# The products of all head chains taken in steps between runs of 24 dense products, with the key norms, decay and rate as a chain of their own

## The chip, the cores and the metric

The kernel runs on one core of a Trainium2 chip. The metric is the device time of one execution in microseconds (us). Engines are named as in the profile: PE is TensorE (matrix products), PEld its weight loads, DVE VectorE, ACT ScalarE, POOL GpSimd, SP SyncE (which here issues the weight transfers). Each engine executes its own instructions strictly in the order in which the program lists them, and waits at an instruction until the data that it names are there.

## The reference

A batch of 256 tokens of width 2048 passes through two transformer blocks in fp32. The first block puts 16 meta tokens in front (T = 272 tokens) and is the one that matters here:

```
proj = rms(h) @ w_in
z_rwkv, z_fox, z_gate = split(proj)
z_rwkv = z_rwkv + (shift(z_rwkv) - z_rwkv) * mu
y_a = rwkv7(z_rwkv, ...)       # 16 heads of 64
y_b = fox(z_fox, ...)          # 16 heads of 64
merged = sig(g_a) * (y_a @ w_a) + sig(g_b) * (y_b @ w_b)
h = h + merged @ w_o
h = h + (silu(gate) * up) @ w_dn
```

rwkv7 is a recurrence over time with a 64x64 state S per head:

```
decay = exp(-exp(-softplus(-(w0 + tanh(wd) @ w2)) - 0.5))
a = sigmoid(a0 + ad @ a2)                     # the rate
kk = (k * k_k) / |k * k_k|                    # keys, normed per head
kf = k * (1 + (a - 1) * k_a)
S = S * decay + (S @ -kk) (kk * a)^T + v kf^T ;  y = S @ r
y = groupnorm(y) + sum(r * kf * r_k) * v ;  y_a = y * (sigmoid(gd) @ g2)
```

fox is causal attention with normed queries and keys and a forget gate that is summed over time and added to the scores before the softmax. The second block (a long convolution, latent attention and another gated feed-forward) isn't touched by the change.

## The kernel before

**Dense products.** Tokens lie along the free axis and features on the partitions. A dense output block (128 features by 256 to 272 tokens) is the sum of 16 k-steps. Each fp32 weight block of 128x128 is split into a high part `wh` and a low part `wl`, and the activations into `xh` and `xl`, so that one k-step is three products (`mm3`, L216 to L218: wh by xh, wl by xh, wh by xl) into one PSUM bank. Weights stream from memory in pieces of eight blocks of 128x128 (one 512 KB transfer on SP's queue into `wr`; ACT copies it to `wh`, L192; DVE subtracts to make `wl`, L193). Each of the three has three buffers.

**Heads.** `phase_heads` makes, for j from 0 to 7, the three projections k, v, r of RWKV head pair j and then its chain (`rwkv_pair`); then fk, fq, fv of fox pair j-1 and its chain (`fox_pair`); and some of the 32 gate blocks (`gate`), by the table GATES_PER_PAIR. The weights come in that order (`in_order`).

The RWKV chain works in five chunks of 64 tokens. From the projections come `p`, `lerp_d` and the shifted `kz`, `zv`, `zr` (L1034 to L1037). The decay and the rate come from two small products on the inputs `twh` and `adh` with weights from `lora` (tiles `sg`, `av`, L1133; the running sum `cc`, L1136; its exponentials `ee` and `ep`, L1140 and L1141), the key norm from a `headsum` (a sum over the 64 rows of a head as a product with a block matrix `bo` or `bm`, L296 and L297; its input is split into a high part `rs_r` on ACT and a low part `rs_q` on DVE). From them DVE makes `kk`, `bk`, `kf`, `ar` (L1149 to L1161) and `t`, which goes into a second headsum, of r, kf and r_k; its result becomes `bv` (L1167). Then come the products of `ar` and `bk` (L1178), the inverse of a triangular matrix in steps of doubling size (L1229, L1235, and `y`/`y5`, L1249 to L1259), and the walk over the five chunks: `rhs` (L1267 to L1271), `uv` (L1274 to L1276), the state `st` (L1280 to L1285) and the output `yc` (L1289 to L1291), with a group norm behind it (two more headsums). All these products are small: 32, 64 or 128 rows and columns of the array, so the array is used in several configurations.

**What sets the order.** The kernel is written one chain after the other. The scheduler of the tile framework lays the instructions of all chains and the dense products out on each engine by readiness and priority; the weight transfers and splits have a raised priority. Nothing in the code says after how many dense products a chain's product comes.

## Time and profile before

| | |
|---|---|
| median of 3 runs | 2821.36 us (2817.64 to 2821.42) |
| profiled execution, its own time | 2817.87 us |
| its span | 2816.1 us |
| mean granted clock of PE | 0.998 |
| PE busy | 2792.4 us (99%), 23296 instructions |
| PEld busy | 2634.0 us (94%) |
| DVE busy | 1845.4 us (66%) |
| ACT busy | 1346.6 us (48%) |
| chain of waits that ended last | PE 95%, DMA 2%, DVE 2%, ACT 1% |

The heads phase is about the first 790 us of the span. Products on PE overlap, so a product's duration (0.28 us for a dense one) isn't what it costs: that is the distance from its start to the next one's start. On DVE and ACT neighbouring instructions overlap by some hundredths of a microsecond, and the durations nearly add up. An execution time is 1.8 us longer than its span in the profile.

### The profile page before, as it was taken

What the parts mean: (1) busy time and instruction counts of PE and PEld (TensorE: products, weight loads), DVE (VectorE), ACT (ScalarE), POOL (GpSimd) and SP (SyncE); (2) the same over time, 40 slices, a digit from 0 to 9 for tenths busy, and PEclk for the clock granted to TensorE, in tenths of its full rate; (3) what the DMA queues carried; (4) which work ended last, traced back from release to release, by engine and by line L of the source; (5) the groups of instructions that cost most, each with busy time, mean ns of one, the idle gap of its engine ahead of it and who ended that gap; (6) DMA issues with size and microseconds to landing.
All of it is one profiled execution on the core that took longest, in us unless ns stands there. A gap on an engine that the chain in (4) does not pass through costs nothing.

```text
span 2816.1 us, 56217 instructions
## 1 busy us (share of the span) xinstructions
PE 2792.4 (99%) x23296; PEld 2634.0 (94%) x23296; DVE 1845.4 (66%) x2958; ACT 1346.6 (48%) x1994; POOL 143.2 (5%) x294
## 2 busy tenths in 40 slices
PE   9999999999999999999999999999999999999998
PEld 9988888888999999999999999999999999998886
DVE  8857667676576665555655556787777777775444
ACT  7545555655444544444444445444454444444443
POOL 0000000010000200000000000000100000000000
PEclk9999999999999999999999999999999999999999
DMA  7333333334576556555556666544555555566554
GB/s 247 128 109 114 105 110 114 104 108 138 180 251 212 193 191 194 194 192 194 194 194 202 201 200 213 165 147 149 190 187 195 194 193 193 195 193 225 193 194 164
DMA packets 147740, 497.13 MB, mean 177 GB/s; under 512 B 16251, under 2 KB 30940, under 8 KB 146908
## 3 DMA queue, kind: packets, MB, share of 16 engines
q1 hardware_dynamic: 128448, 458.42, 49.8%
q10 hardware_dynamic: 18396, 33.03, 3.4%
q8 instruction: 182, 2.98, 0.4%
q0 software_dynamic: 640, 2.10, 0.3%
q14 instruction: 74, 0.61, 0.1%
HBM read 478.27 MB, written 15.20 MB: 175 GB/s over the span
## 4 chain that ended last, share of the span: by engine, by line
PE 95%; DMA 2%; DVE 2%; ACT 1%; issue 0%; DVEq 0%; POOL 0%; ACTq 0%; POOLq 0%
PE psd L218 12%; PE psd L216 12%; PE psd L217 12%; PE psa L217 5%; PE psb L218 5%; PE psb L216 5%; PE psa L218 5%; PE psb L217 5%; PE psa L216 5%; PE psc L217 4%; PE psc L218 4%; PE psc L216 4%; PE psa L962 1%; PE psa L963 1%; PE psa L961 1%; PE psd L963 1%
## 5 line engine op out<-in xcount | busy, mean ns | idle before, releaser
L193 DVE TENSOR_TENSOR wl<-wr,wh 128x1024 fp32r<-128x1024 f32 (+1 forms) x872 | 1062.6, 1219 | 624.3 <-ACT wh L192 623.4
L192 ACT CAST wh<-wr 128x1024 fp32r<-128x1024 f32 (+1 forms) x872 | 908.5, 1042 | 1145.7 <-PE psd L218 328.5
L218 PE MATMUL psd<-xl,wh 128*128 128x256 f32 (+2 forms) x1280 | 370.4, 289 | 0.0
L216 PE MATMUL psd<-xh,wh 128*128 128x256 f32 (+2 forms) x1280 | 369.4, 289 | 0.0
L217 PE MATMUL psd<-xh,wl 128*128 128x256 f32 (+2 forms) x1280 | 368.0, 287 | 0.4 <-DVE wl L193 0.4
L218 PEld LDWEIGHTS psd<-xl,wh 128*128 128x128 f32 x1280 | 240.6, 188 | 7.7 <-issue 2.3
L217 PEld LDWEIGHTS psd<-xh,wl 128*128 128x128 f32 x1280 | 240.7, 188 | 6.6 <-issue 2.2
L216 PEld LDWEIGHTS psd<-xh,wh 128*128 128x128 f32 x1280 | 240.6, 188 | 6.3 <-issue 1.8
L216 PE MATMUL psd<-x3h,wh 128*128 128x256 f32 x496 | 140.3, 283 | 1.6 <-DVE yy L631 1.6
L218 PE MATMUL psd<-x3l,wh 128*128 128x256 f32 x496 | 140.4, 283 | 0.0
L217 PE MATMUL psd<-x3h,wl 128*128 128x256 f32 x496 | 138.6, 279 | 0.0
L216 PE MATMUL psd<-x4h,wh 128*128 128x256 f32 x368 | 100.8, 278 | 3.2 <-ACT x4h L252 3.2
L217 PE MATMUL psd<-x4h,wl 128*128 128x256 f32 x368 | 101.6, 277 | 0.0
L218 PE MATMUL psd<-x4l,wh 128*128 128x256 f32 x368 | 101.2, 277 | 0.0
L262 POOL TENSOR_TENSOR acc<-acc,ssq 128x256 f32<-128x256 f32 x42 | 58.4, 1391 | 822.6 <-ACT ssq L264 818.2
L217 PE MATMUL psa<-x4h,wl 128*128 128x256 f32 x352 | 97.4, 278 | 0.1
L218 PE MATMUL psa<-x2l,wh 128*128 128x256 f32 x352 | 97.4, 277 | 0.0
L216 PE MATMUL psa<-x2h,wh 128*128 128x256 f32 x352 | 97.4, 277 | 0.0
L216 PEld LDWEIGHTS psd<-x3h,wh 128*128 128x128 f32 x496 | 93.1, 188 | 4.5 <-issue 2.8
L218 PE MATMUL psb<-x2l,wh 128*128 128x256 f32 x352 | 97.2, 276 | 0.0
L217 PE MATMUL psb<-x2h,wl 128*128 128x256 f32 x352 | 97.2, 276 | 0.0
L216 PE MATMUL psb<-x2h,wh 128*128 128x256 f32 x352 | 97.2, 276 | 0.0
(673 smaller groups left out, 8384.2 us busy)
## 6 DMA issues: line engine op xcount, KB each, us to landing
wr<-w_in_dram SPq DMA_DIRECT2D x230, 512.0 KB, 3.4
wr<-w_gu_dram SPq DMA_DIRECT2D x176, 512.0 KB, 3.3
wr<-w_down_dram SPq DMA_DIRECT2D x176, 512.0 KB, 3.5
wr<-w_up_dram SPq DMA_DIRECT2D x176, 512.0 KB, 4.3
wr<-w_ab_dram SPq DMA_DIRECT2D x32, 512.0 KB, 4.3
wr<-w_o_dram SPq DMA_DIRECT2D x32, 512.0 KB, 3.4
wr<-w_out_dram SPq DMA_DIRECT2D x32, 512.0 KB, 4.2
spill_g<-acc ACTq DMA_DIRECT2D x32, 128.0 KB, 2.8
```

The costliest lines, as they stand in the source:

```text
L192: self.nc.scalar.copy(hi, src)
L193: self.nc.vector.tensor_tensor(out=lo, in0=src, in1=hi.bitcast(F32), op=ALU.subtract)
L216: nc.tensor.matmul(out, lhsT=wh, rhs=xh, start=start, stop=False)
L217: nc.tensor.matmul(out, lhsT=wl, rhs=xh, start=False, stop=False)
L218: nc.tensor.matmul(out, lhsT=wh, rhs=xl, start=False, stop=stop)
L262: nc.gpsimd.tensor_tensor(out=acc, in0=acc, in1=self.pending[id(acc)], op=ALU.add)
L961: nc.tensor.matmul(ps[b], lhsT=hh[:, k, bs], rhs=wh[:, q], start=k == 0, stop=False)
L962: nc.tensor.matmul(ps[b], lhsT=hh[:, k, bs], rhs=wl[:, q], start=False, stop=False)
L963: nc.tensor.matmul(ps[b], lhsT=hl[:, k, bs], rhs=wh[:, q], start=False, stop=k == HT - 1)
```

## The change

Every chain becomes a generator that stops at each place where a product would have to wait for another engine. `dense` counts k-steps, and after every TICK = 8 of them (24 dense products) it calls `tick`, which lets every live chain take one step. An `issue_after` holds these steps behind the dense product that was just written, and a `hold` keeps the next dense product behind all of them. So PE's order is written out: 24 dense products, one step of each chain, 24 dense products, and so on. The chains are:

- `rwkv_early` (new): the key norm, the two products for decay and rate (now in bank "a", not "b"), and the exponentials. It starts with the k projection of its pair, ahead of v and r.
- `rwkv_pair`: the rest; it starts behind the r projection. The transposes of `zv` come at its start. Where each chunk had the product of `ka` with `v` accumulate with that of `ar` and the state in one bank, the products of all five chunks are now made at once, copied by ACT into `kv` (L1342), and DVE adds `kv` to the state's product (L1385) where it copied before. `outer` (the product for `yc`) comes one step later.
- two `headnorm` chains per fox pair and `fox_heads`; the products with `v` move a step later, into bank "a".

`headsum` takes its bank itself and stops between the split of its input and its two products: for one step, or for two with gap=1 (the key norm and fox norms; the sum that makes `bv` and the two of the group norm have no gap). GATES_PER_PAIR goes from (2, 0, 2, 3, 3, 2, 2, 2, 0) to (5, 2, 3, 2, 3, 2, 3, 5, 0), and the weight stream with it. The forget gates move behind the last gate block of j = 0.

```diff
+TICK = 8
     def dense(self, out, st, kt, xh, xl, tok):
         for k in range(kt):
             wh, wl = next(st)
-            self.mm3(out, wh, wl, xh[:, k, tok], xl[:, k, tok], k == 0, k == kt - 1)
+            with ExitStack() as held:
+                for i in self.hold:
+                    held.enter_context(self.tc.issue_after(i))
+                m = self.mm3(out, wh, wl, xh[:, k, tok], xl[:, k, tok], k == 0, k == kt - 1).ins
+            self.hold = []
+            self.since += 1
+            if self.chains:
+                self.hold = [m]
+                if self.since >= TICK:
+                    self.since = 0
+                    self.tick(m)
+
+    def tick(self, ins):
+        for c in list(self.chains):
+            with self.tc.issue_after(ins):
+                if next(c, self) is self:
+                    self.chains.remove(c)
+        traced = self.nc.cur_bb.bb.instructions
+        at = next(k for k in reversed(range(len(traced))) if traced[k] is ins)
+        self.hold = [i for i in traced[at:] if i.engine == ins.engine]
...
-    def headsum(self, ps, w, src, n, pool=None):
+    def headsum(self, bank, w, src, n, pool=None, gap=0):
         self.split(src, hi, lo)
+        for _ in range(gap + 1):
+            yield
+        ps = self.ps(bank)[:, :n]
         self.nc.tensor.matmul(ps, lhsT=w, rhs=hi, start=True, stop=False)
         self.nc.tensor.matmul(ps, lhsT=w, rhs=lo, start=False, stop=True)
+        return ps
...
         nc.vector.scalar_tensor_tensor(out=t1[:, 64:], in0=zr[:, 64:], scalar=self.col("r_k", j), in1=kf[:, 64:], op0=ALU.mult, op1=ALU.mult)
-        ps = self.ps("b")[:, :S]
-        self.headsum(ps, self.bo, t1[:, 64:], S)
+        yield
+        for c0, n in ((0, 3), (3, 2)):
+            ps = self.ps("a").rearrange("p (c x) -> p c x", c=4)
+            for c in range(n):
+                nc.tensor.transpose(ps[:, c], zv[:, 64 * (c0 + c) : 64 * (c0 + c) + 128], self.con("ident"))
+            nc.scalar.copy(uv[64:128, c0 : c0 + n], ps[64:128, :n])
+            nc.vector.tensor_copy(v0[:64, c0 : c0 + n], ps[64:128, :n, 0:64])
+        ps = yield from self.headsum("b", self.bo, t1[:, 64:], S)
...
+            if c:
+                yield
+                rhs = self.tl(w2, [P, 64], "rhs")
+                ps = self.ps("c")
+                for hs in hss:
+                    nc.tensor.matmul(ps[hs, :64], lhsT=ar[hs, c, 0], rhs=st[hs], start=True, stop=True)
+                nc.vector.tensor_tensor(out=rhs, in0=ps[:, :64], in1=kv[:, c], op=ALU.add)
+                if c > 1:
+                    outer(c - 1, old)
+                yield
+                inner(c, rhs)
```

Below are the places at which the order of the engines changes most for what follows. Rows stand in an engine's order; names are tiles, with their buffer numbers.

**The headsum of r, kf and r_k in pair 2.** Its input is `t`, split into `rs_r` and `rs_q`; `psb` takes the sum. First PE before: the product of the low part stands 15 rows behind that of the high part (the first row).

```order
L296 MATMUL psb_2449<-rs_r_2450,bo_472 128x256
...
L216 MATMUL psd_3941<-xh_94,wh_3973 128x256
L217 MATMUL psd_3941<-xh_94,wl_3974 128x256
L297 MATMUL psb_2449<-rs_q_2451,bo_472 128x256
L1274 MATMUL psc_1780<-rhs_1778,xtf_1594 64x64 x2
L218 MATMUL psd_3941<-xl_95,wh_3973 128x256
```

And DVE before, up to that low part:

```order
L1163 SCALAR_TENSOR_TENSOR t_489_2439<-zr_48_431,cols_61,kf_2440 128x256
L1192 TENSOR_SCALAR bs_2489<-bk_2437,ed_2490 128x128 x4
L193 TENSOR_TENSOR wl_4026<-wr_4024,wh_4025 128x8x128
L193 TENSOR_TENSOR rs_q_2451<-t_489_2439,rs_r_2450 128x256
L1271 COPY rhs_1778<-psc_1773 128x64
```

Now PE has the same two products directly behind the state product L1384 of another pair's walk:

```order
L219 MATMUL psd_2641<-xl_95,wh_2693 128x272
L1384 MATMUL psc_2702<-st_2654,ar_1559 64x64 x2
L334 MATMUL psb_2706<-rs_r_2667,bo_472 128x256
L335 MATMUL psb_2706<-rs_q_2668,bo_472 128x256
L217 MATMUL psd_2641<-xh_94,wh_2693 128x272
```

And DVE now:

```order
L1256 COPY v_482_2628<-psa_2662 64x128
L1097 SCALAR_TENSOR_TENSOR zr_48_431<-lerp_d_2623,cols_61,p_2622 128x256
L1420 TENSOR_TENSOR yc_1524<-yc_1524,psc_2575 128x256
L1385 TENSOR_TENSOR rhs_2701<-psc_2702,v_258_1557 128x64
L194 TENSOR_TENSOR wl_2790<-wr_2788,wh_2789 128x8x128
L1247 TENSOR_TENSOR ar_2630<-zr_48_431,ee_2459 128x5x64
L1249 SCALAR_TENSOR_TENSOR t_485_2631<-zr_48_431,cols_61,kf_2632 128x256
L194 TENSOR_TENSOR rs_q_2668<-t_485_2631,rs_r_2667 128x256
L1259 TENSOR_TENSOR bv_2709<-psb_2706,zv_47_430 128x256
```

The low part `rs_q` moved from ahead of `rhs` to four rows behind it, and `rhs` reads the product (`psc_2702`) that stands directly ahead of the headsum on PE. In pairs 1 to 7 the row ahead is such a reader of the same step each time: `rhs` in pairs 1, 2, 4 and 6, the state `st` in pairs 3, 5 and 7.

**ACT at the end of a matrix inverse.** Before (pairs 4 and 5), the copy of `y` stands between the tanh of `sg` and of `av`:

```order
L1275 COPY uv_4656<-psc_4835 64x64
L1133 ACT_TABLE_LOAD
L1133 ACTIVATE sg_441<-psb_5686,half_427 128x272
L1252 COPY y_988_4807<-psa_4806 32x128
L1133 ACTIVATE av_442<-psb_5692,half_427 128x272
L1141 ACTIVATE ep_5702<-cc_5698 128x320
L192 CAST wh_6471<-wr_6470 128x8x128
L1140 ACTIVATE ee_5701<-cc_5698 128x640
L1259 COPY xtf_4689<-psa_4818 32x4x32
```

Now (pairs 3 and 4), the copies `kv` (named `v` here, L1342) and `y` stand behind all of the next pair's early chain:

```order
L355 ACTIVATE rs_r_4634<-rs_v_4633 128x320
L1421 DMA spill_ya<-yc_3612 128x256
L193 CAST wh_5664<-wr_5663 128x256
L356 ACTIVATE rs_q_4635<-rs_r_4634 128x320
L1215 ACT_TABLE_LOAD
L1215 ACTIVATE av_442<-psa_4648,half_427 128x272
L1223 ACTIVATE ep_4658<-cc_4654 128x320
L1222 ACTIVATE ee_4657<-cc_4654 128x640
L193 CAST wh_4811<-wr_4810 128x8x128
L193 CAST gh_5701<-wr_5700 128x256
L1342 COPY v_713_3754<-psc_4698 128x320
L1350 COPY y_919_4711<-psa_4710 32x128
```

And on PE their readers (L1365 needs `kv`, L1355 needs `y`) stand one run of 24 dense products behind the step that made those copies' inputs:

```order
L219 MATMUL psd_4688<-xl_95,wh_4744 128x258
L1365 MATMUL psc_4764<-v_713_3754,xtf_4068 64x64 x2
L1355 MATMUL psa_4752<-xtf_4068,y_919_4711 32x32 x8
L217 MATMUL psd_4688<-xh_94,wh_4744 128x258
```

So `kv` and `y` moved on ACT from the middle of the next pair's tanh and exponentials to behind them and behind two weight splits, and the next step on PE reads them. Pairs 0, 1, 3 and 5 have this overlap with the next pair's early chain.

**The start, pair 0.** Here the headsum of the key norm and that of r, kf and r_k are 23 dense products apart on PE now (from the first row to the last but one):

```order
L335 MATMUL psb_694<-rs_q_651,bo_472 128x320
L217 MATMUL psd_654<-xh_94,wh_686 128x258
...
L219 MATMUL psd_766<-xl_95,wh_813 128x256
L334 MATMUL psb_821<-rs_r_787,bo_472 128x256
L335 MATMUL psb_821<-rs_q_788,bo_472 128x256
```

DVE has 17 rows between the result of the first (`rs_v`) and the low part for the second (`rs_q_788`), of which these are the last twelve:

```order
L194 TENSOR_TENSOR wl_895<-wr_893,wh_894 128x8x128
L1097 SCALAR_TENSOR_TENSOR zr_48_431<-lerp_d_748,cols_61,p_747 128x256
L1241 TENSOR_TENSOR t_126_756<-kk_697,av_442 128x320
L1246 SCALAR_TENSOR_TENSOR ar_755<-kk_697,ee_722 128x5x64
L1247 TENSOR_TENSOR ar_755<-zr_48_431,ee_722 128x5x64
L1242 TENSOR_TENSOR bk_754<-t_126_756,ep_723 128x5x64
L1243 TENSOR_SCALAR t_126_756<-av_442,cols_61 128x320
L1244 SCALAR_TENSOR_TENSOR kf_757<-t_126_756,kz_46_429 128x320
L1245 TENSOR_TENSOR bk_754<-kf_757,ep_723 128x5x64
L1249 SCALAR_TENSOR_TENSOR t_126_756<-zr_48_431,cols_61,kf_757 128x256
L1271 TENSOR_SCALAR bs_831<-bk_754,ed_832 128x128 x4
L194 TENSOR_TENSOR rs_q_788<-t_126_756,rs_r_787 128x256
```

Before, the scheduler had put 13 us of the trace between these two headsums (65.07 to 78.78 us of the span, from the product of the first to the split for the second).

More of the change, by code (lines that the diff above doesn't have):

```diff
@@ L234, in dense, with chain, drain @@
             wh, wl = next(st)
-            self.mm3(out, wh, wl, xh[:, k, tok], xl[:, k, tok], k == 0, k == kt - 1)
+            with ExitStack() as held:
[17 more added lines that the diff above has]
+        self.hold = [i for i in traced[at:] if i.engine == ins.engine]
+    def chain(self, c):
+        next(c)
+        self.chains.append(c)
+        return c
+    def drain(self, chains):
+        for c in chains:
+            for _ in c:
+                pass
+            if c in self.chains:
+                self.chains.remove(c)
     def group(self, out, st, kt, xh, xl, toks, bring):
@@ L511, in headnorm @@
         nc.scalar.activation(out=sq, in_=z, func=AF.Square)
-        ps = self.ps("b")[:, :n]
-        self.headsum(ps, self.bo, sq, n, w)
+        ps = yield from self.headsum("b", self.bo, sq, n, w, gap=1)
         zn = self.tl(w2, [P, T], tag + "n")[:, :n]
@@ L1086, in phase_heads @@
             self.fox_setup(pr)
+            pairs, fox = [], None
             for j in range(9):
                 if j < 8:
[L1089 to L1091 removed]
+                    box = self.rwkv_inputs(j)
+                    self.drain(pairs[-2:-1])
+                    pairs.append(self.chain(self.rwkv_pair(j, w, box)))
                 if j:
[L1093 to L1095 removed]
+                    if j == 1:
+                        with self.tc.issue_after(behind):
+                            self.forget_gates()
+                    self.drain(fox)
+                    fox = [self.fox_pair(j - 1)]
+                else:
+                    fox = []
+                for i in range(GATES_PER_PAIR[j]):
+                    behind = self.gate().ins
             while self.ngate < 32:
                 self.gate()
+            self.drain(list(self.chains))
     def gate_inputs(self):
@@ L1244, in rwkv_pair @@
                 nc.gpsimd.tensor_copy(xf[:, 0], xt[:, 0])
+        yield
+        ps = self.ps("c")[:, : NC5 * 64].rearrange("p (c t) -> p c t", c=NC5)
+        for c in range(NC5):
+            for h, hs in enumerate(hss):
+                kat, vv = (ka[:, c], v0[:64, c]) if h == 0 else (gs[1][64:128, c, 0], uv[64:128, c, 64:128])
+                nc.tensor.matmul(ps[hs, c], lhsT=kat, rhs=vv, start=True, stop=True)
+        kv = v0
+        nc.scalar.copy(kv, ps)
         ps = self.ps("a")[:, :P].rearrange("p (c t) -> p c t", c=4)
```

163 lines of the change are left out of this document (92 added, 71 removed).

## The prediction

> **What bounds the kernel now.** I read the page's busy shares first, then the chain of waits, then busy time by stretch, to see whether PE has any room in the heads phase.
>
> ```profile
> PE 2792.4 (99%) x23296; PEld 2634.0 (94%) x23296; DVE 1845.4 (66%) x2958; ACT 1346.6 (48%) x1994; POOL 143.2 (5%) x294
> PE 95%; DMA 2%; DVE 2%; ACT 1%; issue 0%; DVEq 0%; POOL 0%; ACTq 0%; POOLq 0%
> ```
>
> ```profile
> core 0: us, PE busy (x) PEld busy (x) DVE busy (x) ACT busy (x) POOL busy (x), PEclk, DMA share, GB/s
> 30.00:70.00 40.00, 40.00 (x329) 39.92 (x328) 36.70 (x69) 30.82 (x44) 1.04 (x7) 1.00 0.62 200
> ...
> 70.00:200.00 130.00, 129.67 (x1223) 115.89 (x1224) 88.98 (x184) 63.99 (x114) 11.34 (x17) 1.00 0.36 118
> 200.00:500.00 300.00, 300.00 (x2798) 259.27 (x2797) 211.56 (x484) 162.45 (x315) 22.77 (x34) 1.00 0.34 111
> 500.00:800.00 300.00, 299.60 (x2691) 265.89 (x2691) 193.50 (x400) 162.18 (x293) 22.63 (x24) 1.00 0.45 144
> ```
>
> PE never stands still in the phase: 0.7 us of idle time in the 730 us from 70 to 800, at a granted clock of 1.00. The change can therefore gain only by making PE's own sequence shorter, and whatever it makes PE wait is lost one for one. DVE is busy for 65 to 70% of each stretch (91% in the first), so it has slack on average, and none to spare for a wait of a fixed length.
>
> What PE spends beyond products shows in PE's timeline around one visit to the chains:
>
> ```profile
> 301.16 0.28 PE L217 MATMUL psd<-xh,wl 128*128 128x258 f32 x1
> 301.28 0.28 PE L218 MATMUL psd<-xl,wh 128*128 128x258 f32 x1
> 301.49 0.27 PE L1267 MATMUL psc<-v,ka 64*64 64x64 f32 x1
> ...
> 303.91 0.29 PE L297 MATMUL psb<-rs_q,bo 128*128 128x272 f32 x1
> 304.04 0.28 PE L216 MATMUL psd<-xh,wh 128*128 128x258 f32 x1
> ```
>
> A dense product costs 0.12 us from start to start (301.16 to 301.28); going from it to a 64*64 product costs 0.21 (to 301.49). A headsum, 128*128 like the dense ones, is left for 0.13. So what costs is the change of the array's shape, about 0.09 us on entry. The Trainium skill ("TensorEngine Tiling (Array Packing)", Key Properties) says that switching the tiling mode drains TensorE; the rows agree, with 0.09 us as the price here. By that rule too the change gains only by its count of switches.
>
> **The change part by part.** *Fewer visits.* The order of PE's instructions has 282 runs of dense products before and 154 now, 146 of them of exactly 24; changes of array shape fall from 853 to 721. The number of dense and of chain products stays (4032 and 1729). 132 changes fewer at 0.09 us would be 12 us. Half of them are ways back, and the one that the rows show costs 0.01 (0.13 for 0.12): 66 x 0.09 + 66 x 0.01 = 7. I take -8 us, with -6 and -12 as ends.
>
> *Pinned places.* Before, a chain's product stood wherever its data were ready. Now it stands 24 dense products (24 x 0.12 = 2.9 us) and a step's small products behind the last one, ready or not. What DVE and ACT must do between two steps has to fit into that. The durations, with the groups of DVE and ACT from 70 to 786 us:
>
> ```profile
> L193 DVE TENSOR_TENSOR wl<-wr,wh 128x1024 fp32r<-128x1024 f32 (+1 forms) x154 | 185.0, 1201 | 61.0 <-ACT wh L192 60.3
> L1271 DVE COPY rhs<-psc 128x64 f32<-128x64 f32 x40 | 8.8, 220 | 14.2 <-PE psc L1269 12.7 <-PE psc L1267 0.9
> L1161 DVE TENSOR_TENSOR ar<-zr,ee 128x320 f32<-128x320 f32 x7 | 3.4, 479 | 0.6 <-ACT ee L1140 0.6
> L1163 DVE SCALAR_TENSOR_TENSOR t<-zr,cols,kf 128x256 f32<-128x256 f32 x8 | 3.8, 477 | 0.0
> L193 DVE TENSOR_TENSOR rs_q<-t,rs_r 128x256 fp32r<-128x256 f32 x8 | 3.3, 413 | 0.0
> L1285 DVE SCALAR_TENSOR_TENSOR st<-st,ed,psc 128x64 f32<-128x64 f32 x24 | 6.7, 278 | 6.8 <-PE psc L1280 6.3
> L1192 DVE TENSOR_SCALAR bs<-bk,ed 128x128 f32<-128x128 f32 x32 | 7.0, 277 | 0.0
> ```
>
> ```profile
> L192 ACT CAST rs_r<-t 128x256 fp32r<-128x256 f32 x8 | 3.2, 403 | 3.4 <-DVE t L1163 3.2 <-ACT uv L1275 0.2
> L1133 ACT ACT_TABLE_LOAD x4 | 5.1, 1283 | 0.1
> L1133 ACT ACTIVATE av<-psb,half 128x272 f32<-128x272 f32 x7 | 3.4, 483 | 0.2
> L317 ACT ACTIVATE rs_q<-rs_r 128x256 f32<-128x256 f32 (+2 forms) x31 | 13.4, 433 | 0.6
> L1141 ACT ACTIVATE ep<-cc 128x320 f32<-128x320 f32 x7 | 3.3, 471 | 3.5 <-DVE cc L1136 3.4
> L1140 ACT ACTIVATE ee<-cc 128x640 f32<-128x640 f32 x7 | 5.1, 732 | 0.0
> L192 ACT CAST wh<-wr 128x1024 fp32r<-128x1024 f32 (+1 forms) x153 | 156.0, 1021 | 121.9 <-PE psd L218 109.8 <-issue 6.1 <-DMA wr<-w_in_dram 2.7
> L1240 ACT COPY xt<-psa 128x320 f32<-128x320 f32 x24 | 10.3, 427 | 7.8 <-DVE xn L1237 7.4
> L1252 ACT COPY y<-psa 32x128 f32<-32x128 f32 x8 | 2.1, 259 | 0.3
> ```
>
> *(a) The headsum of r, kf and r_k, pairs 1 to 7.* It has no gap, and DVE's rows in the changed order show the trouble: the low part it needs stands behind `rhs`, and `rhs` reads the product directly ahead of it on PE. So PE finishes L1384 and then waits while DVE does `rhs` 0.22, a weight split 1.20, `ar` 0.48 and `t` 0.48, ACT the high part 0.40, DVE the low part 0.41: 3.2 us, with no room for anything beside. Four pairs (1, 2, 4, 6) are so. In pairs 3 and 5 it is `st` 0.28, four `bs` 1.11, a split 1.20 and 0.41: 3.0 us (the high part lies beside). In pair 7 `st`, a split and the low part: 1.9 us. Sum 4 x 3.2 + 2 x 3.0 + 1.9 = 20.7, say +21 us. Before, the same rows cost PE nothing, because the low part's product stood behind other dense products:
>
> ```profile
> 299.34 1.22 DVE L193 TENSOR_TENSOR wl<-wr,wh 128x1024 fp32r<-128x1024 f32 x1
> 300.48 0.87 DVE L1192 TENSOR_SCALAR bs<-bk,ed 128x128 f32<-128x128 f32 x4
> ...
> 301.68 0.41 DVE L193 TENSOR_TENSOR rs_q<-t,rs_r 128x256 fp32r<-128x256 f32 x1
> ```
>
> Here neighbours start 5 to 10% closer than their durations add up to (1.14 for 1.22), so the lower end is 18. The upper end has DVE late at `rhs` too, by one more weight split in each pair: 21 + 7 x 1.2 = 29. What is late behind it is the next weight split, which the wait itself gives time for.
>
> *(b) `kv` and `y`, pairs 0, 1, 3 and 5.* From the tanh of `sg` to the copy of `y` ACT has in order: tanh 0.48, table 1.28, root 0.47 (put at that of `ep`, of the same shape), a small split 0.40, the second part of the root 0.43, table 1.28, tanh 0.48, exponentials 0.47 and 0.73, a weight split 1.02, a small split 0.40, `kv` 0.43 (as the copy of the same shape at L1240), `y` 0.26: 8.1 us. PE comes back for it after two runs of dense products and one step, 5.8 + about 1 = 6.8 us. DVE's half of `y` is later still: behind the second tanh (4.8 us in) it has `av`, `kk` twice, `p`, `lerp_d`, `t` and `ar`, seven rows that I put at `ar`'s 0.48 at most (3.2 together, with `av` shorter), then a weight split 1.20 and `y` 0.28, which ends at 9.5. That makes 1.3 to 2.7 us each; I take 2, +8 us; the ends are 0 (a table load that is not needed, a split done earlier) and 12.
>
> *(c) The start, pair 0.* The headsums of key norm and of r, kf, r_k are 23 dense products apart, 2.8 us. The trace of before has the same work on DVE:
>
> ```profile
> 65.07 0.31 PE L297 MATMUL psb<-rs_q,bo 128*128 128x320 f32 x1
> ```
>
> ```profile
> 65.42 0.49 DVE L315 TENSOR_SCALAR rs_v<-psb 128x320 f32<-128x320 f32 x1 [1.03 <-PE psb L297]
> 65.97 1.23 DVE L193 TENSOR_TENSOR wl<-wr,wh 128x1024 fp32r<-128x1024 f32 x1
> 68.26 0.49 DVE L321 SCALAR_TENSOR_TENSOR rs_q<-rs_q,rs_v 128x320 f32<-128x320 f32 x1 [1.06 <-ACT rs_q L317]
> ...
> 78.78 0.41 DVE L193 TENSOR_TENSOR rs_q<-t,rs_r 128x256 fp32r<-128x256 f32 x1
> ```
>
> It took 14.1 us (65.07 to 79.19). Three fewer weight splits lie between now (3 x 1.14 = -3.4), none of the next pair's six input rows (6 x 0.4 = -2.4), and three such rows for `zr` come in (+1.2): 9.5, less the 2.8 that PE has: 6.7. I take +7 us, with 4 and 9 as ends.
>
> *Parts I cost at nothing.* The kat-by-v products at once and `kv`'s copy are the same products and one ACT copy in (b). Two more table loads (54 for 52 in the order of ACT) are 2.6 us on ACT, busy for half of the phase. The new order of gates moves weights that arrive well ahead; SP has no other work in between, and the transfers of 512 KB keep their count. If that cover were gone, each late piece would cost one split, 1.2 us.
>
> *Sum.* -8 + 21 + 8 + 7 = +28 us on the profiled execution of 2817.87 (span 2816.1 and 1.8 around it): 2846. The median before, 2821.36, is 3.5 above its profiled execution; I set the median of the changed kernel 2 above mine: 2848 us.
>
> **The rivals.** *Waits hidden, only the switches count (faster).* The steps would meet their data as before, and the -8 us would stand alone: 2821 - 8 = 2813. Place: the seven headsums of (a). For it: DVE is idle for a third of the phase. Against it: the order on DVE is fixed, and the row ahead reads PE's product of the same step, so no idle time before it helps. It decides if each wait in (a) is below 1 us with (b) and (c) near nothing.
>
> *Gain and waits cancel (same).* (a) at 1.2 us each, one split, because `ar` and `t` find their inputs early and the splits overlap: 7 x 1.2 = 8, against -8, with (b) and (c) near zero: 2821. For it: `t` itself doesn't need the split. Against it: the split stands ahead of it in DVE's order.
>
> *The clock drops (slower by more).* Each of some eight waits of over 3 us would let PE go on at half pace for a while; a run of 24 dense products at half pace costs another 2.9 us: 8 x 2.9 = 23, so 2871. Against it: the granted clock is 1.00 in every stretch above, but none has a wait as long. The Trainium skill ("TensorE: Matmul & The Clock Gate", Part 1) says that about 3.4 us of idle time bring the clock to half rate, and as long a busy time brings it back; by it (c) alone surely qualifies and those of (a) are at the edge. No run here shows it.
>
> *The ticks don't do what they say.* If order on PE were not held, times would stay within 0.2%; the 146 runs of exactly 24 speak against it, so I fold it into "same".
>
> **How the numbers follow.** Forecast 0.72; clock drop 0.12; same 0.08; hidden 0.08. The forecast's ends: all terms at their lowest, -12 + 18 + 0 + 4 = +10, give 2828 to 2830; all at their highest, -6 + 29 + 12 + 9 = +44, give 2862 to 2864. The range 2824 to 2866 holds these with 2 to 4 us for the spread of runs; the clock case and most of the two others lie outside. A change of 0.2% (5.6 us) is about what a measurement of this kernel can tell from none: slower by more than that 0.84 (forecast and clock drop), within it 0.08, faster 0.08.
>
> **What would show it.** In the profile after, PE's idle time between 30 and 790 us rises from below 1 us to about 36. In the groups, L335 on `rs_q`/`bo` (or L334) shows some 20 us of idle time ahead with DVE's or ACT's split as its releaser, L1355 or L1365 some 8 with `y`, `xtf` or `v0`. The start shows one wait of about 7 us near 60 to 75 us. Entries into 64*64 products still cost 0.21, and are fewer. DVE and ACT busy time stay within 1%. I am wrong if PE stays above 99.5% busy in the phase, if the idle time is ahead of weight splits (L217 on `wl`) instead, or if the granted clock falls.

## The result, and the profile after

The changed kernel takes 2861.84 us (median of 4 runs, 2858.97 to 2865.47) against 2819.5 us for the kernel before on the same chip (4 runs, 2813.83 to 2821.42). The ratio is 1.0156, with a 95% interval of 1.0143 to 1.0168. It is 42 us slower; the forecast was 2848 us, 28 us slower, with a range of 2824 to 2866, near whose upper end the result lies.

The page of the changed kernel, busy shares and the chain of waits:

```profile
PE 2798.3 (98%) x23296; PEld 2647.8 (92%) x23296; DVE 1840.9 (64%) x2950; ACT 1354.1 (47%) x2004; POOL 149.3 (5%) x294
PE 90%; DVE 4%; ACT 2%; DMA 2%; issue 1%; ACTq 0%; POOL 0%; DVEq 0%; POOLq 0%
```

The work of each engine is what it was (DVE 1845 to 1841 us, ACT 1347 to 1354), and the span went from 2816.1 to 2863.7. PE's share of the chain fell from 95% to 90%, and DVE's and ACT's grew. Busy time by stretch (each row: length, then busy time and number of instructions of PE, PEld, DVE, ACT, POOL, then PE's granted clock, DMA share and GB/s) shows where:

```profile
30.00:70.00 40.00, 28.02 (x201) 27.08 (x200) 32.03 (x69) 21.00 (x33) 0.81 (x7) 0.84 0.40 136
70.00:200.00 130.00, 126.36 (x1217) 115.17 (x1216) 80.83 (x162) 65.33 (x115) 13.94 (x15) 0.97 0.36 119
200.00:500.00 300.00, 283.69 (x2591) 250.91 (x2590) 195.74 (x442) 156.78 (x295) 21.41 (x30) 0.97 0.34 110
500.00:800.00 300.00, 289.35 (x2643) 256.12 (x2644) 187.98 (x411) 156.52 (x297) 25.86 (x28) 0.98 0.37 121
```

PE is idle for 12.0 + 3.6 + 16.3 + 10.7 = 42.6 us here; before it was 0.7. The granted clock, 1.00 in every stretch before, is below 1. What PE lost by that while busy is 28.0 x 0.16 + 126.4 x 0.03 + 283.7 x 0.03 + 289.4 x 0.02 = 22.6 us. What PE waited for, from 30 to 840 us (total, times, longest):

```profile
PE psb L334 <- ACT rs_r L193: 20.2, 9, 8.0
PE psb L335 <- DVE rs_q L194: 6.8, 7, 1.8
PE psa L217 <- ACT sg L1215: 4.7, 4, 1.4
PE psa L1254 <- ACT ep L1223: 3.9, 1, 3.9
PE psc L1365 <- issue: 2.1, 2, 1.3
PE psa L1355 <- DVE y L1349: 2.1, 2, 1.2
PE psc L1365 <- ACT v L1342: 1.0, 1, 1.0
```

27 us of it are headsums (L334 and L335): 8.0 at the start in pair 0, 18.2 at the headsum of r, kf and r_k in pairs 1 to 7. Here is pair 2, first PE's timeline, then DVE's:

```profile
221.81 0.28 PE L219 MATMUL psd<-xl,wh 128*128 128x272 f32 x1
222.02 0.33 PE L1384 MATMUL psc<-st,ar 64*64 64x64 f32 x4
225.59 0.58 PE L334 MATMUL psb<-rs_r,bo 128*128 128x256 f32 x1 [3.23 <-ACT rs_r L193]
226.04 0.58 PE L335 MATMUL psb<-rs_q,bo 128*128 128x256 f32 x1
226.43 0.43 PE L217 MATMUL psd<-xh,wh 128*128 128x272 f32 x1
226.65 0.43 PE L218 MATMUL psd<-xh,wl 128*128 128x272 f32 x1
```

```profile
222.95 0.22 DVE L1385 TENSOR_TENSOR rhs<-psc,v 128x64 f32<-128x64 f32 x1
223.08 1.22 DVE L194 TENSOR_TENSOR wl<-wr,wh 128x1024 fp32r<-128x1024 f32 x1
224.21 0.48 DVE L1247 TENSOR_TENSOR ar<-zr,ee 128x320 f32<-128x320 f32 x1
224.62 0.48 DVE L1249 SCALAR_TENSOR_TENSOR t<-zr,cols,kf 128x256 f32<-128x256 f32 x1
225.57 0.42 DVE L194 TENSOR_TENSOR rs_q<-t,rs_r 128x256 fp32r<-128x256 f32 x1 [0.47 <-ACT rs_r L193]
```

PE makes L1384 and then waits 3.23 us, while DVE ends the row ahead, does `rhs`, a weight split, `ar` and `t`, and ACT makes the high part. The last two PE rows show something else: after the wait a dense product costs 0.22 us (226.43 to 226.65), not 0.12. That is the clock, from the same view by stretch for the changed kernel behind two of these waits:

```profile
225.00:227.00 2.00, 1.41 (x5) 1.24 (x6) 0.85 (x3) 0.41 (x1) 0.00 (x0) 0.50 0.73 260
227.00:229.00 2.00, 2.00 (x11) 2.00 (x10) 0.09 (x1) 0.00 (x0) 0.00 (x0) 0.50 0.01 2
408.00:410.00 2.00, 2.00 (x13) 2.00 (x12) 0.04 (x1) 0.00 (x0) 0.00 (x0) 0.64 0.64 242
410.00:412.00 2.00, 2.00 (x10) 1.79 (x8) 0.44 (x1) 0.47 (x1) 0.00 (x0) 0.51 0.00 0
```

The granted clock falls to a half. There are eleven such falls in the phase (they begin at 50, 64, 139, 204, 224, 303, 395, 409, 501, 579 and 665 us), each in a wait or behind one. They last 3.4 or 6.8 us, the one at 64 us 10.2 us with most of the wait inside, and each costs 1.7 to 3.0 us.

**The books.** Span +47.6 = idle time +42 and lost clock +23 less some 17 us: PE's own sequence did become shorter, by more than the 8 us of the prediction.

### The profile page after: what moved, and what is told of

Same layout as the page of the kernel before. It is cut to its first block, busy times and chain, and to the rows that moved or that the text cites. A ratio compares the mean times of both kernels' runs of the same rounds, so it can differ in the third digit from the quotient of the medians.

```text
span 2863.7 us, 56190 instructions
## 1 busy us (share of the span) xinstructions
PE 2798.3 (98%) x23296; PEld 2647.8 (92%) x23296; DVE 1840.9 (64%) x2950; ACT 1354.1 (47%) x2004; POOL 149.3 (5%) x294
## 4 chain that ended last, share of the span: by engine, by line
PE 90%; DVE 4%; ACT 2%; DMA 2%; issue 1%; ACTq 0%; POOL 0%; DVEq 0%; POOLq 0%
PE psd L217 11%; PE psd L219 11%; PE psd L218 11%; PE psa L218 4%; PE psa L217 4%; PE psb L219 4%; PE psb L218 4%; PE psa L219 4%; PE psb L217 4%; PE psc L218 4%; PE psc L219 4%; PE psc L217 4%; PE psa L1021 1%; PE psa L1022 1%; PE psa L1023 1%; PE psd L1022 1%
## 5 line engine op out<-in xcount | busy, mean ns | idle before, releaser
L193 ACT CAST wh<-wr 128x1024 fp32r<-128x1024 f32 x872 | 909.9, 1044 | 1229.1 <-PE psd L219 412.7
L194 DVE TENSOR_TENSOR wl<-wr,wh 128x1024 fp32r<-128x1024 f32 x872 | 1062.9, 1219 | 615.7 <-ACT wh L193 615.2
L217 PE MATMUL psd<-xh,wh 128*128 128x256 f32 (+2 forms) x1280 | 382.5, 299 | 0.1
L217 PEld LDWEIGHTS psd<-xh,wh 128*128 128x128 f32 x1280 | 249.1, 195 | 11.3 <-issue 5.3
L218 PEld LDWEIGHTS psd<-xh,wl 128*128 128x128 f32 x1280 | 249.8, 195 | 0.0
L219 PEld LDWEIGHTS psd<-xl,wh 128*128 128x128 f32 x1280 | 249.4, 195 | 0.0
L219 PE MATMUL psc<-x2l,wh 128*128 128x256 f32 x352 | 97.2, 276 | 0.0
```

The costliest lines, as they stand in the source:

```text
L193: self.nc.scalar.copy(hi, src)
L194: self.nc.vector.tensor_tensor(out=lo, in0=src, in1=hi.bitcast(F32), op=ALU.subtract)
L217: nc.tensor.matmul(out, lhsT=wh, rhs=xh, start=start, stop=False)
L218: nc.tensor.matmul(out, lhsT=wl, rhs=xh, start=False, stop=False)
L219: return nc.tensor.matmul(out, lhsT=wh, rhs=xl, start=False, stop=stop)
```

## The experiments

Each ratio is against the kernel before, measured beside the run on the same chip. The median of the kernel before was 2816.8 us beside the first four rows, 2817.77 beside the next four and 2816.43 beside the last two.

| run | edit | median us | ratio (95%) |
|---|---|---|---|
| e_gap | headsum of r, kf, r_k one step later | 2834.17 | 1.0062 (1.0047 to 1.0077) |
| e_bank | decay and rate in bank b | 2864.01 | 1.0170 (1.0155 to 1.0185) |
| e_fill | the waits of (a) filled with products | 2856.99 | 1.0142 (1.0126 to 1.0158) |
| e_gates | kernel before, new table of gates | 2821.80 | 1.0018 (1.0009 to 1.0028) |
| e_lora | both products ahead of the tanh | 2862.08 | 1.0161 (1.0144 to 1.0177) |
| e_start | more steps for pair 0 | 2859.98 | 1.0149 (1.0134 to 1.0164) |
| e_free1 | e_gap + e_lora + e_start | 2825.36 | 1.0029 (1.0019 to 1.0039) |
| e_free2 | e_free1, kv/y and the headsum a step later | 2822.84 | 1.0019 (1.0010 to 1.0028) |
| e_best | each wait taken away at its cause | 2793.55 | 0.9921 (0.9906 to 0.9936) |
| e_ab | decay in bank a, rate in bank b | 2851.32 | 1.0123 (1.0106 to 1.0140) |

### e_gap: the headsum of r, kf and r_k one step later

```diff
-        ps = yield from self.headsum("b", self.bo, t1[:, 64:], S)
+        ps = yield from self.headsum("b", self.bo, t1[:, 64:], S, gap=1)
...
-        yield
         for h in range(2):
             yield
```

> One part of the change undone in effect: the headsum of r, kf and r_k takes its products one step later (gap=1), and a bare step behind it goes, so that the chain has as many steps as before. Theory 1 (pinned waits): the seven waits of pairs 1 to 7 (PE starts 2.8 to 4.4 us late at each in the trace of the change, 22 us in all) go, and with them the four falls of the granted clock that follow them (at 138, 225, 408 and 501 us, 1.7 to 3.0 us lost at each, 9 in all): 2862 - 31 = 2831 us. Pair 0 keeps most of its 8 us. Rival (the wait moves): the low part is late one step later too, or another tile of the chain is: half of it, 2846 us.

2834.17 us, where theory 1 said 2831 and the rival 2846. What is left of PE's waits for the headsum in the profile:

```profile
PE psb L334 <- ACT rs_r L193: 7.7, 2, 6.6
PE psa L217 <- ACT sg L1215: 4.7, 4, 1.4
PE psa L1254 <- ACT ep L1223: 3.7, 1, 3.7
```

From nine waits of 20.2 us two are left, that of pair 0 (6.6) and one of 1.1 us in pair 2, which still waits 0.9 us more for `rs_q`. So the seven waits come from where these products were pinned, and one step more is enough in six of the seven pairs. The mend takes back some 27 us of the 42 us (1.0156 to 1.0062), but not by the terms of theory 1. In the profiled execution, the slowest of the four, PE's idle time from 30 to 800 us fell from 42.6 to 25.5 us. The four falls of the clock are gone, but two new ones stand at 467 and 770 us and others became longer, so the lost clock fell only from 22.6 to 20.2 us instead of by 9. The rest of the 28.5 us of span isn't assigned.

### e_fill: the same waits filled with products

Ahead of the headsum, and held behind all other products of the step, PE makes 20 products more whose result is overwritten.

```diff
         ps = self.ps(bank)[:, :n]
+        if fill:
+            last = [i for i in self.nc.cur_bb.bb.instructions if i.engine == self.pe][-1]
+            with self.tc.issue_after(last):
+                for _ in range(fill):
+                    self.nc.tensor.matmul(ps, lhsT=w, rhs=self.gdh[:, 0, :n], start=True, stop=True)
         self.nc.tensor.matmul(ps, lhsT=w, rhs=hi, start=True, stop=False)
...
-        ps = yield from self.headsum("b", self.bo, t1[:, 64:], S)
+        ps = yield from self.headsum("b", self.bo, t1[:, 64:], S, fill=20)
```

> Ahead of the headsum of r, kf and r_k and behind all other products of that step, PE makes 20 products of 128x128 by 256 whose result is overwritten (20 x 0.12 = 2.4 us), in all eight pairs. The waits' ends are set by DVE and ACT, so PE's work must not cost time where it waits longer than that. Theory 1 (idle time brings the clock down): PE idles below 1.2 us at these seven places, the granted clock stays at 1.00 behind them, and the 1.7 to 3.0 us lost behind four of them come back: 2862 - 9 = 2853 us. Rival (the clock falls for another reason, such as the small products of the chains before it): the clock falls as before and the time is 2862 us or, where a wait was shorter than the filling, up to 2 above.

2856.99 us: PE does 160 products more and the kernel is no slower than the changed one: 4.9 us faster by the medians, with ratios whose intervals overlap (1.0142 and 1.0156), and 8.9 us by the spans of the profiled executions (2854.8 for 2863.7). The same stretches as above, of this run:

```profile
225.00:227.00 2.00, 2.00 (x18) 2.00 (x17) 0.14 (x1) 0.00 (x0) 0.00 (x0) 1.00 0.09 29
227.00:229.00 2.00, 2.00 (x19) 1.80 (x18) 0.98 (x2) 1.59 (x3) 0.00 (x0) 1.00 0.00 0
408.00:410.00 2.00, 2.00 (x18) 1.87 (x16) 1.11 (x3) 0.83 (x2) 0.00 (x0) 1.00 0.23 47
410.00:412.00 2.00, 2.00 (x15) 1.53 (x14) 1.72 (x3) 0.72 (x2) 0.00 (x0) 1.00 0.57 223
```

The clock stays at 1.00 where it had fallen to a half, and 18 or 19 products fit into 2 us behind the first wait where there were 5 and 11. Of the eleven falls, six are left, none of them behind one of the seven filled waits. The lost clock is 13.6 us for 22.6, as much less as the span. So the clock at these places falls for want of products and not because of what stands ahead of the wait. By the medians about half of the 9 us that were expected came back; the runs of this kernel lie 10 us apart (2850 to 2861), so the trace shows the clock's part and the times alone would not.

The run doesn't show that idle time alone counts. Three pairs of neighbouring stretches of 3.41 us, two of the changed kernel and one of e_gap, say more:

```profile
299.32:302.73 3.41, 2.03 (x26) 1.70 (x23) 2.67 (x8) 2.32 (x5) 0.00 (x0) 1.00 0.43 153
302.74:306.15 3.41, 3.41 (x17) 3.41 (x17) 1.40 (x3) 3.35 (x5) 0.00 (x0) 0.50 0.28 82
480.23:483.64 3.41, 2.03 (x16) 1.81 (x15) 2.67 (x8) 2.79 (x6) 0.00 (x0) 1.00 0.50 156
483.64:487.05 3.41, 3.41 (x31) 3.20 (x30) 0.94 (x3) 3.37 (x5) 0.00 (x0) 1.00 0.23 77
```

```profile
767.01:770.42 3.41, 3.41 (x26) 2.13 (x24) 1.68 (x3) 1.70 (x4) 0.00 (x0) 1.00 0.49 180
770.42:773.83 3.41, 3.41 (x14) 2.71 (x13) 1.66 (x8) 1.17 (x5) 0.00 (x0) 0.50 0.34 130
```

The same idle time (1.38 us of 3.41) is followed by a fall at 303 us and by none at 484 us, and at 770 us the clock falls behind a stretch without any idle time. What differs is how many columns PE's products put out, counted from their shapes (a dense product has 256 to 272, most small ones 32 to 128). The products that start in the first stretch of each pair have 3056, 3536 and 2880 columns in sum. In each trace the falls begin whole multiples of 3.41 us apart. Cut into intervals by these beats, the twelve profiles have, from 30 to 790 us, 74 falls out of the full clock. All 74 follow an interval of at most 3232 columns; 25 intervals of so few had no fall behind them, and none of the 2466 intervals with more had one (the median interval in the kernel before has 5888). So too few columns in such an interval go with a fall, be it for a wait or for small products.

### e_bank and e_lora: two failed reasons for the wait at the rate

PE waits in four pairs (0.9 to 1.7 us from start to start) between the product for the decay and that for the rate, until ACT's tanh `sg` has read the first. The first idea was the bank's letter, which the change had moved from "b" to "a":

```diff
-            ps = self.ps("a")[:, :T]
+            ps = self.ps("b")[:, :T]
             self.mm3(ps, lh[:, i], ll[:, i], xh, xl, True, True)
```

> One part of the change undone: the two products for decay and rate take bank b again, not bank a. Theory: in the trace of the change the second of these products waits 0.9, 1.7, 1.7 and 1.7 us (pairs 2, 3, 5 and 7), because its bank is the one that ACT's copy of xtf still reads, behind a table load and the tanh of the first product. With bank b these 5.9 us go, and the falls of the clock behind three of them (203, 302 and 664 us, 1.7 each): 2862 - 11 = 2851 us. Rival: bank b is as late, because the key norm and the fox scores use it: no change, 2862 us.

2864.01 us: no gain, the rival was right. The second was the order in which the products and the tanh are written:

```diff
-            ps = self.ps("a")[:, :T]
-            self.mm3(ps, lh[:, i], ll[:, i], xh, xl, True, True)
+            two.append(self.ps("a")[:, :T])
+            self.mm3(two[i], lh[:, i], ll[:, i], xh, xl, True, True)
+        for i, out in enumerate((sg, av)):
+            ps = two[i]
```

> The changed kernel with one edit: the products for decay and for rate are both written (each into a bank of its own) ahead of the tanh that reads the first. With bank b in place of bank a the waits of 0.9 to 1.7 us at the second product stayed, and they end with ACT's tanh of the first product, so the reason can't be the bank's neighbour. Theory: the second product is put into the bank that this tanh still reads, behind a table load. With both written first the four waits go (6 us) and the falls of the clock behind three of them (1.7 us each, 5): 2862 - 11 = 2851 us. Rival: the second product's bank comes free as late from another reader: 2862 us.

2862.08 us: no gain again. The waits in the profiles of e_bank and of e_lora, one row each:

```profile
PE psb L217 <- ACT sg L1215: 6.6, 5, 1.9
```

```profile
PE psa L217 <- ACT sg L1218: 4.7, 4, 1.4
```

### e_ab: two letters

The built program of the changed kernel gives the two products one and the same bank in pairs 2, 3, 5 and 7 (the traces don't show banks). A letter has two banks in this kernel; in these pairs the other is held by `xtf`'s or the key norm's tile, whose reader stands behind the tanh. So neither the letter nor the order of writing could help, and two letters should.

```diff
-            ps = self.ps("a")[:, :T]
+            ps = self.ps("ab"[i])[:, :T]
             self.mm3(ps, lh[:, i], ll[:, i], xh, xl, True, True)
```

> The changed kernel with one edit: the product for the decay in bank a, the one for the rate in bank b. In the built program of the changed kernel both lie in one and the same bank in pairs 2, 3, 5 and 7, since the other bank of that letter was still held by a tile whose reader comes later; writing both first did not alter this. Theory: the second product no longer waits for the tanh of the first; its 6 us of waits go and the falls of the clock behind three of them (5 us): 2862 - 11 = 2851 us. Rival: what is late behind them (the headsum two steps on, kv and y) takes it up: 2860 us.

2851.32 us, as the theory said (2851). The row with `sg` is gone from the waits; what is left, in its first rows:

```profile
PE psb L334 <- ACT rs_r L193: 27.1, 8, 8.3
PE psb L335 <- DVE rs_q L194: 4.1, 4, 1.4
PE psa L1254 <- DVE zv L1097: 3.4, 1, 3.4
```

The headsums took up some of it (31 us for 27), and the falls of the clock went from eleven to eight. That makes the sum of 11 us right by its terms only in part: idle time 42.6 to 39.1 and lost clock 22.6 to 17.0 make 9 us, and that the time met the theory's to 0.3 us is luck.

### e_start: more room for pair 0

```diff
-        yield
+        for _ in range(3 if j == 0 else 1):
+            yield
...
-        ps = yield from self.headsum("b", self.bo, t1[:, 64:], S)
+        ps = yield from self.headsum("b", self.bo, t1[:, 64:], S, gap=3 if j == 0 else 0)
...
-GATES_PER_PAIR = (5, 2, 3, 2, 3, 2, 3, 5, 0)
+GATES_PER_PAIR = (7, 2, 3, 2, 3, 2, 3, 3, 0)
```

> Pair 0 alone gets more room: two steps more ahead of its transposes of zv and three more between the split and the products of its headsum of r, kf and r_k; two more gate blocks at the start (two fewer at pair 7) give these steps dense products to stand behind. Theory: the waits of 4.2 us (zv not there yet) and 8.3 us (the low part behind 17 rows of DVE) at the start go, and the two falls of the clock behind them (2.3 and 2.6 us): 2862 - 17 = 2845 us. Rival: the start is bound by DVE as a whole (it was 91% busy there before), and the wait comes back at the next products, ar by bk: half of it, 2854 us.

2859.98 us, 2 us for the 17 expected, and not clear of the noise (ratios 1.0149 and 1.0156, intervals overlapping). The waits at the start went from 12 us to some 5. But new waits come up at other places (1.4 and 1.7 us in pair 1 near 119 and 133 us, 2.7 us at 397), and behind the phase, with two gate blocks fewer at its end, the next one waits for its first input:

```profile
PE psa L1356 <- DVE y L1350: 4.9, 3, 2.5
PE psa L217 <- ACT yah L193: 4.8, 1, 4.8
```

The last row is new: `yah` is the input of the merge behind the heads phase. It stays in e_free1 and e_free2, which have the same table, and is gone in e_best, which has five gate blocks at the end again. The gain was given back at other pinned places.

### e_gates: the table of gates alone, in the kernel before

```diff
-GATES_PER_PAIR = (2, 0, 2, 3, 3, 2, 2, 2, 0)
+GATES_PER_PAIR = (5, 2, 3, 2, 3, 2, 3, 5, 0)
```

> The kernel before with the changed table of gates per pair and the weight order that follows from it, nothing else. I cost this part at nothing: PE is packed in the heads phase and the scheduler fills as before: within 5 us of the kernel before. Rival: the order of gates carries part of the loss or gain, 5 to 10 us either way, for instance because five gates at the start cover the first chain: faster by up to 5.

2821.80 us for 2816.8: 0.18% slower, no wait of PE beyond 0.6 us and no fall of the clock. It is within the 5 us that were costed at nothing.

### e_free1 and e_free2: the mends together

e_free1 is e_gap, e_lora and e_start in one kernel (pair 0 with gap=4).

> The three mends together in the changed kernel: the headsum of r, kf and r_k one step later, both products for decay and rate ahead of the tanh, more room for pair 0. What is left of the waits is that of kv and y and their neighbours. Theory 1 (a visit saved is worth 0.15 us): the books of the run with the late headsum leave 23 us of gain once idle time and lost clock are taken off, so 129 fewer visits are worth about 20 us, and the time is 2818 - 20 + what its own profile shows of idle time and lost clock (some 10 and 7): 2805 to 2818 us. Theory 2 (8 us, as predicted): the same sum gives 2817 to 2830 us.

2825.36 us. That lies inside the range of theory 2 and 7 us above that of theory 1, but both ranges put 17 us in for idle time and lost clock. Its profile shows 23 and 7 us from 30 to 800 us, because of the 4.7 us at `yah` and of the waits that e_lora leaves:

```profile
PE psa L217 <- ACT sg L1218: 5.8, 5, 1.4
PE psa L217 <- ACT yah L193: 4.7, 1, 4.7
PE psa L1358 <- DVE y L1352: 3.6, 3, 1.2
```

With these 30 us theory 1 gives 2828 and theory 2 2840 us, so the run speaks for theory 1. So do the books of the phase alone: the heads phase, from the first dense product of the pairs to the first of the merge, is as long as before (753.8 for 754.5 us), although it holds 18 us of idle time and 5 us of lost clock. So the sequence itself is some 23 us shorter.

e_free2 adds a step between the copies of `kv` and `y` and their readers, and one at the headsum:

```diff
         nc.scalar.copy(y5[96:128], ps[96:128])
         yield
+        yield
```

> As the run with the three mends, with one step more between the copies of kv and y and the products that read them, and one more at the headsum of r, kf and r_k. Theory: the waits of kv and y in pairs 0, 3 and 5 (6 us in the changed kernel) and the two falls of the clock behind them (3.4 us) go as well: 5 to 9 us below the run with the three mends. Rival: the chains have no steps to spare, and what is late moves on to the products by the state (st, rhs): no difference, or slower by up to 5 us.

2822.84 us, 2.5 us below e_free1: less than theory and more than rival. The waits at `y` go, but the same products (L1359) wait 2.0 us for DVE's copy `v`, three waits of up to 2.2 us come at the first `uv` product (L1369), which now shares bank c with the group norm of the pair before, and the wait at `yah` grows to 6.3 us.

### e_best: each wait taken away at its cause

On top of the late headsum (gap=2), the step behind `y` and the room for pair 0:

```diff
-GATES_PER_PAIR = (5, 2, 3, 2, 3, 2, 3, 5, 0)
+GATES_PER_PAIR = (7, 2, 2, 2, 2, 2, 3, 5, 0)
...
-            ps = self.ps("a")[:, :T]
+            ps = self.ps("ab"[i])[:, :T]
             self.mm3(ps, lh[:, i], ll[:, i], xh, xl, True, True)
...
         def inner(c, rhs):
-            ps = self.ps("c")
+            ps = self.ps("b" if c == 0 else "c")
```

> The changed kernel with every wait found so far taken away where its cause lies: the headsum of r, kf and r_k two steps behind its split; one step more between kv, y and their readers; pair 0 with two steps more ahead of its transposes and its headsum five steps behind the split; the product for the rate in bank b and that for the decay in bank a; the first uv product in bank b (it shared bank c with the group norm of the pair before); gates per pair 7, 2, 2, 2, 2, 2, 3, 5. PE keeps 150 runs of dense products (282 before). Theory 1 (a visit saved is worth 0.15 us): with some 5 us of idle time left and no fall of the clock, 2818 - 132 x 0.15 + 5 = 2803 us. Theory 2 (visits worth 8 us in all): 2815 us. Rival: the chains have no steps to spare and the end of the phase waits for the last pair, as it did for 5 us with the three mends: 2808 us by theory 1.

2793.55 us, 0.9921 of the kernel before (0.9906 to 0.9936): 23 us faster than before, 68 below the change, and 9 below what theory 1 gave: a visit saved was worth more than its 0.15 us. Its stretches:

```profile
30.00:70.00 40.00, 38.13 (x312) 37.42 (x311) 35.55 (x68) 27.43 (x40) 0.80 (x7) 1.00 0.50 173
70.00:200.00 130.00, 128.20 (x1293) 117.33 (x1293) 92.21 (x185) 72.13 (x129) 13.18 (x17) 1.00 0.39 135
200.00:500.00 300.00, 300.00 (x2955) 269.61 (x2950) 219.01 (x495) 163.21 (x326) 24.78 (x34) 1.00 0.36 121
500.00:780.00 280.00, 277.12 (x2544) 249.77 (x2541) 186.06 (x386) 150.31 (x279) 19.30 (x24) 1.00 0.43 144
```

The clock is 1.00 throughout the phase, PE's idle time 6.6 us, and in the 300 us from 200 to 500 PE makes 2955 products where the kernel before made 2798, without a gap in either. With the waits gone a large gain is left, which the part on the sum lays to the fewer changes of the array's shape. The phase is 725.7 us long, 28.8 less than before, with 6 us of idle time in it, so the sequence is about 35 us shorter, 0.27 us for each of 132 visits saved.

## Why the prediction was right, and where its sum was not

**What bounds: right.** PE's waits cost their full length. DVE and ACT did the same work, and their share of busy time told nothing.

**(a) The pinned headsum, +21 us: right in place and cause, near in size.** The starts of PE's products lie 2.8 to 3.7 us apart at these seven places, 22 us in all, of which some 2 would be there anyway; PE's idle time there is 18.2 us. Pair 2 has the rows of the working (0.22, 1.22, 0.48 and 0.48 on DVE, then ACT's high part), but that its wait of 3.23 us meets the 3.2 of the sum is in part luck: DVE reached `rhs` only 0.6 us after PE's product, since `yc` (L1420) stood ahead of it, and the low part's 0.41, counted in the sum, came when PE had already started again. In pairs 1, 4 and 6 DVE made `ar` and `t` ahead of the split and ACT's high part ran beside it: 2.2 to 2.5 us of idle time for the 3.2. Pairs 3, 5 and 7 had 2.7, 3.0 and 2.3 for 3.0, 3.0 and 1.9. e_gap shows the cause: these waits go with one step more, but for 2.0 us in pair 2.

**(b) kv and y, +8 us: 5 us.** 2.1 at L1355 and 3.1 at L1365. It is in pairs 0, 3 and 5 and hardly in pair 1, within the ends of 0 and 12.

**(c) The start, +7 us: 8.0 us at the headsum; the transposes missed.** The wait of 3.9 us at L1254, where `zv` is not ready, wasn't in the sum. (The row above names ACT's `ep`, which ends at about the same time; the transposes read `zv`, done at 52.2 us, and the profiles of e_ab and e_bank name it.) The order would have shown it by the same reading: PE has three dense products between the products for decay and rate and these transposes.

**What I cost at nothing** hid the four waits at the rate (4.7 us): back to back, the two products fell into one bank, and in e_ab, with two letters, these waits are gone. Together idle time came to 42 us for the 36 forecast.

**The clock, a rival at 0.12, is the first term that failed.** It was priced at 23 us and held apart from the forecast, with the argument that no stretch of the trace before had a fall. The stretches of that trace had no waits either, so they could say nothing. The profile shows 22.6 us of lost clock in addition to the waits. It was no rival; it belongs in the sum beside the waits. One of the prediction's own signs of being wrong, a fall of the granted clock, came true. That 22.6 is so near the rival's 23 is luck: the rival had eight waits of over 3 us at 2.9 each, and there were eleven falls of 1.7 to 3.0, six of them with shorter waits.

**Fewer visits, -8 us, is the second: 132 changes of shape at 0.06 us.** Counted over the records of the phase, changes of the array's shape fall from 799 to 696 in the changed kernel and to 646 in e_best. From before to e_best, intervals across a change fall by 31.8 us in sum (146.1 to 114.3), and 146 intervals more without a change cost nothing more: 35 us for 153, 0.23 us each if all of it is laid to them. I had taken the way back at 0.01 from one row, and that row left a headsum, which has the dense products' shape. The timeline of before shows a way back from a small one:

```profile
367.57 0.28 PE L1269 MATMUL psc<-st,ar 64*64 64x64 f32 x2
367.78 0.39 PE L216 MATMUL psd<-xh,wh 128*128 128x256 f32 x1
368.01 0.28 PE L217 MATMUL psd<-xh,wl 128*128 128x256 f32 x1
368.12 0.28 PE L218 MATMUL psd<-xl,wh 128*128 128x256 f32 x1
```

The first dense product takes 0.23 us to the next (367.78 to 368.01), the second 0.11. In the records of before that is so in 202 of the 253 returns that two or more dense products follow: in all 189 behind a small shape, and in 13 of the 64 behind a 128*128 product. At 0.23 each, the 103 changes fewer of the records are -24 us in the changed kernel (the prediction's 132 were counted in the program's order; why the counts differ isn't shown). The sum with the measured terms is -24 + 42 + 23 = +41, for +47.6 us of span and +42 us by the medians. Some 6 us of the span are not settled; the records have waits below 0.6 us that I haven't assigned. A count by entries agrees in part: PE goes from 128*128 to a smaller shape 279 times before, 209 in the changed kernel and 196 in e_best. One way in and out costs 0.09 us on entry, 0.10 on the way back (0.15 for 0.05 between small products of one shape) and 0.11 at the first dense product, 0.30 in all. That gives 21 us in the changed kernel, and 25 of the 35 us in e_best; where the other 10 come from isn't shown.

So the total was near by luck: two errors, 16 us of gain not counted and 23 us of clock held apart, largely offset each other. The waits were no luck; they were read from the order.

**The rivals.** "Waits hidden" and "same" fell with (a): the order on DVE was fixed, as argued. Had the waits been hidden, the gain would have been about 24 us, not 8.

## What to carry to other kernels

A product pinned at a fixed distance behind others waits for whatever stands ahead of its operand on the other engine: read from the order whether that engine reads a product of the same step first, and give such an operand one step more. Price a wait of a packed PE at its length and add what the clock loses. Here that was 22.6 us beside 42.6 us of idle time, but 20.2 beside 25.5 in e_gap and 5 beside 18 in the phase of e_free1: it went by the columns put out in an interval of 3.41 us and not by each wait. Price a change of the array's shape over a whole visit, from the last dense product ahead to the second one behind, and not on one row. When a mend moves a step, look again at every place where it now meets another chain; here the mends gave 27, 10, 2 and 0 us alone, and the kernel with a mend at each cause 68 us.

## What the runs showed of the hardware that was not expected

Waits of 0.9 us (at 203 us) to 1.7 us were enough for the granted clock to fall to 0.50, and not only waits of 3.2 us and above. Pair 3's wait of 1.66 us from start to start at 302 us has a fall behind it in the changed kernel and in e_bank and e_lora, while a wait of the same length at 482 us has none in the changed kernel and one in e_bank and e_lora. So a single wait's length doesn't decide it. The intervals of 3.41 us shown under e_fill do better: the clock fell only behind intervals of at most 3232 columns, once (at 770 us in e_gap) without any idle time; why 25 such intervals had no fall isn't settled here. Each short fall costs 1.7 us, that is 3.4 us at half clock. The Trainium skill ("TensorE: Matmul & The Clock Gate", Part 1) gives about 3.4 us of busy time until the clock is back, which these rows agree with; its 3.4 us of idle time until it falls is more than some waits here had.

The first dense product behind small ones costs about twice a later one (0.20 to 0.24 for 0.12 us), in all 189 such returns before; a way in and out costs here 0.09, 0.10 and 0.11 us. The Trainium skill's rule that switching the tiling mode drains TensorE ("TensorEngine Tiling (Array Packing)", Key Properties) was weighed in the prediction by the way in alone.
